# Weight tiles moved to 64 bytes beside the activation tiles, and the start of a hybrid decoder trunk put in another order

## The chip, the cores and the metric

The kernel runs on one core of one Trainium2 chip. The metric is device microseconds for one execution, from the launch on the device to its end. Lower is better.

## What is computed

Two layers of a decoder trunk over 256 positions of width 1024. Each layer makes a normed and conditioned h out of x, sends it through one large input projection, runs three branches (a gated linear recurrence, dilated window attention with rotary positions, gated linear attention), projects each back to the width, gates and adds them, and adds the product with `w_o` to x:

```python
mod = c_act @ ada_w + ada_b
shift, scale, gate = jnp.split(mod, 3, axis=-1)
h = rmsnorm(x, norm_g) * (1.0 + scale[:, None]) + shift[:, None]
z = h @ w_in
(a_x, a_g, b_q, b_k, b_v, b_g, c_q, c_k, c_v, c_g, m_g) = jnp.split(z, ...)
ya = rg_lru(causal_dwconv(a_x, conv_w, conv_b), lru_wa, lru_ba, lru_wx, lru_bx, lru_lambda)
ya = ya * jax.nn.silu(a_g)
q = rope(rmsnorm(b_q.reshape(shp), qn_g[:, None, :]), pos) * (HEAD_DIM ** -0.5)
k = rope(rmsnorm(b_k.reshape(shp), kn_g[:, None, :]), pos)
...
merged = mg[:, :, 0] * (ya @ proj_a) + mg[:, :, 1] * (yb @ proj_b) + mg[:, :, 2] * (yc @ proj_c)
return x + gate[:, None] * (merged @ w_o)
```

`rmsnorm` divides by the root of the mean square over the width; `rg_lru` uses softplus of a parameter; `rope` needs the cosine and sine of position times frequency. All weights are float32; with the conditioning weights `ada_w` they make up nearly all of the 168 MB that are read, each once.

## The kernel before

**Products.** To keep float32 accuracy, each factor is split into two parts in TensorE's rounded format: `whi` and `wlo` for weights, `hhi` and `hlo` for h, `yhi` and `ylo` for the branch results, `mhi` and `mlo` for the merged one. Every product is three matmuls into the same place (hi x hi, lo x hi, hi x lo). In the form of L797 to L799 (helper `mm_f`, 256 moving columns) the weights are loaded into the array and the activations stream; so also in L777 to L779 (gate of attention, `bg`). In the form of L789 to L791 (helper `mm_t`, 384, 400 or 512 moving columns) the activations are loaded and the weights stream; for q, k and v the loaded activations are every second column (`x[:, k, t::2]`).

**Units.** The weights come in units of up to 512 KB, 288 of them over two layers, in the order of a string: `a0 q1 k1 v1 k2 q2 v2 a1 q3 k3 v3 mA pA c0 c1 c2 c3 mC pC mB pB wo`, ahead of which q, k, v of pair 0 and bg run together. `advance` (from L206) keeps three units ahead: SP's queue loads `raw`, ACT makes `whi` (L223), DVE makes `wlo` (L224). Six `raw` buffers and four each of `whi` and `wlo` are in the pool `wts`. The rows of `ada_w` come between the units and are reduced on DVE (`ada_tile`, L325); at the start, sixteen of them come between the first units, since h needs them.

**Memory.** Tiles are laid out in SBUF pool after pool, in the order in which the pools are made: `one`, then `two`, then `wts`. By the addresses of the build, modulo 128 bytes: `whi` and `wlo` begin at 64; `hhi` and `hlo` (and `mhi` and `mlo`, under the same tags) at 32; `yhi` and `ylo` at 0.

**The start.** SP's queue issues the loads of `c_sb`, the identity, x in two halves, `vec_sb` (small vectors) and then the weights. ACT and DVE make `cact` (the SiLU of the conditioning), DVE `diag`, TensorE turns it into a row that stands on all partitions (L313), ACT copies it to `crow`, which `ada_tile` needs. `stats_start` squares x on ACT (four instructions, L372), adds on DVE (L375, L376) and sums over partitions with two matmuls of ones (L379). `rstd_full` makes the inverse root with a logarithm and an exponential on ACT and one Newton step on DVE (L341 to L348). `h_tile` makes h, eight tiles, each as soon as its two rows of `ada_w` are reduced (L357 `tmp`, L359 `hhi`, L360 `hlo`). The angles, sines and rotary tables of layer 0 (`angles`, `rope_tables`, L412 to L442) are asked for at unit 2 and wait for the last h tile written so far, `softplus` (L390 to L404) at unit 16; the loads that they need are issued on SP's queue behind unit loads. The order of instructions on each engine is that of a scheduler that models time, within these bounds.

Of the kernel before, what the change touches and what calls it, by code (L numbers as in the profile page):

```python
# [12 lines left out]
I32 = mybir.dt.int32  # L13
# [113 lines left out]
def hybrid_trunk(ctx: ExitStack, tc: tile.TileContext, ws, ada, vec, gates, a2, qkg, c_t, x_t, pos, inv, eye,  # L127
# [107 lines left out]
    pos_sb = one.tile([P, 2], I32, name="pos_sb")  # L235
# [21 lines left out]
    epsc = one.tile([P, 1], F32, name="epsc")  # L257
    V.memset(epsc, EPS)
    mhalf = one.tile([P, 16], F32, name="mhalf")
    V.memset(mhalf, -0.5)  # L260
    hpi = one.tile([P, 1], F32, name="hpi")
    V.memset(hpi, float(np.pi / 2))
    att_sb = one.tile([P, 3, P], F32, name="att_sb")
    G.memset(att_sb, 0.0)

# [33 lines left out]
    cact = one.tile([P, KT], F32, name="cact")  # L299
# [18 lines left out]
    mod = one.tile([P, L, 3, KT], F32, name="mod")  # L318
    acc = one.tile([P, L, 24], F32, name="acc")
# [31 lines left out]
    def h_alloc(l):  # L351
        return one.tile([P, KT, S], F32R, name="hhi", tag="hhi"), one.tile([P, KT, S], F32R, name="hlo", tag="hlo")
# [15 lines left out]
    def stats_start():  # L368
        sq = []
        for i, tag in enumerate(("cv", "csg", "co", "bv")):  # L370
# [12 lines left out]
    sp4 = one.tile([P, L, KT], F32, name="sp4")  # L383
    sp4n = one.tile([P, L, KT], F32, name="sp4n")
    hb = one.tile([P, L, 2 * KT], F32, name="hb")

    def softplus():
        lam = vec_sb[:, :, V_LAM:V_LAM + KT]
        e, s, s2, p = (one.tile([P, L, KT], F32, name=f"spl{i}") for i in range(4))
# [20 lines left out]
    def angles():  # L410
        pf, an, k = (one.tile([P, 2] if i == 0 else [P, 2, 32], F32, name=f"an{i}") for i in range(3))
# [128 lines left out]
    def evac_qk(l, nm, p, ps):  # L540
        i = 0 if nm == "q" else 1
        ro = two.tile([P, 2, 6, 64], F32, name="ro")
        ss = two.tile([P, 2, 6], F32, name="ss")
# [420 lines left out]
    def small():  # L964
        a, v = cur["h_last"]
        with tc.issue_after(a), tc.issue_after(v):
            softplus()
# [103 lines left out]
```

## Time and profile before

| | |
|---|---|
| three runs | 910.75, 912.31, 912.46 us; median 912.31 |
| the profiled execution | 912.47 us, of which span 910.7 us |
| granted TensorE clock, mean | 0.996 of full |
| TensorE (PE) busy | 872.9 us, 96% of the span, 6,340 matmuls |
| VectorE (DVE) busy | 673.0 us, 74% |
| ScalarE (ACT) busy | 532.0 us, 58% |
| GpSimd (POOL) busy | 175.1 us, 19% |
| read from HBM | 168.23 MB, 186 GB/s over the span |

The busy share says which engine has the least room. How long one matmul occupies the engine when others follow it is not its duration, since they are pipelined, but the distance from its start to the next start. The timeline (start, duration, engine, line, operation, tiles, and in brackets the idle time before it and what ended that) tells both. The view by windows gives busy time and counts of each engine in a stretch of the span.

### The profile page before, as it was taken

What the parts mean: (1) busy time and instruction counts of PE and PEld (TensorE: products, weight loads), DVE (VectorE), ACT (ScalarE), POOL (GpSimd) and SP (SyncE); (2) the same over time, 40 slices, a digit from 0 to 9 for tenths busy, and PEclk for the clock granted to TensorE, in tenths of its full rate; (3) what the DMA queues carried; (4) which work ended last, traced back from release to release, by engine and by line L of the source; (5) the groups of instructions that cost most, each with busy time, mean ns of one, the idle gap of its engine ahead of it and who ended that gap; (6) DMA issues with size and microseconds to landing.
All of it is one profiled execution on the core that took longest, in us unless ns stands there. A gap on an engine that the chain in (4) does not pass through costs nothing.

```text
span 910.7 us, 16407 instructions
## 1 busy us (share of the span) xinstructions
PE 872.9 (96%) x6340; PEld 825.3 (91%) x6340; DVE 673.0 (74%) x1115; ACT 532.0 (58%) x897; POOL 175.1 (19%) x160
## 2 busy tenths in 40 slices
PE   3989999999999999999999999989999999999998
PEld 3978999999988888999889999989999988899998
DVE  6998898669666667666775888986896666656674
ACT  4376976686644554634454689666874545554451
POOL 0026365124000110100030525551330001000000
PEclk9999999999999999999999999999999999999999
DMA  9884456446765666676655544563667565455651
GB/s 328 317 279 139 145 165 207 132 136 201 240 189 191 202 212 205 208 238 206 224 152 160 177 145 145 179 195 109 190 206 232 160 190 163 150 173 185 188 163 47
DMA packets 52111, 170.16 MB, mean 187 GB/s; under 512 B 6240, under 2 KB 8160, under 8 KB 52032
## 3 DMA queue, kind: packets, MB, share of 16 engines
q1 hardware_dynamic: 51216, 167.04, 57.7%
q10 hardware_dynamic: 672, 1.87, 0.7%
q8 instruction: 50, 0.82, 0.4%
q0 software_dynamic: 144, 0.20, 0.2%
q14 instruction: 29, 0.24, 0.1%
HBM read 168.23 MB, written 1.05 MB: 186 GB/s over the span
## 4 chain that ended last, share of the span: by engine, by line
PE 57%; DVE 18%; DMA 10%; issue 7%; ACT 5%; POOL 3%; SPq 0%; DVEq 0%; ACTq 0%
PE mm L797 10%; PE mm L799 10%; PE mm L798 10%; DMA raw<-in_ada_dram 8%; DVE wlo L224 7%; PE mm L791 6%; PE mm L790 6%; PE mm L789 6%; PE xps L172 1%; ACT whi L223 1%; POOL ss L560 1%; PE xps L168 1%; DVE raw L325 1%; DVE rb L554 1%; DVE ra L552 1%
## 5 line engine op out<-in xcount | busy, mean ns | idle before, releaser
L224 DVE TENSOR_TENSOR wlo<-raw,whi 128x1024 fp32r<-128x1024 f32 (+2 forms) x288 | 335.6, 1173 | 86.9 <-ACT whi L223 85.5
L223 ACT CAST whi<-raw 128x1024 fp32r<-128x1024 f32 (+2 forms) x288 | 280.2, 977 | 189.5 <-PE mm L798 123.6
L797 PE MATMUL mm<-hhi,whi 128*128 128x256 f32 x768 | 217.8, 284 | 3.3 <-DVE rb L554 3.2
L799 PE MATMUL mm<-hhi,wlo 128*128 128x256 f32 x768 | 216.6, 282 | 3.1 <-DVE wlo L224 3.1
L798 PE MATMUL mm<-hlo,whi 128*128 128x256 f32 x768 | 216.0, 281 | 0.0
L789 PE MATMUL mm<-whi,hhi 128*128 128x384 f32 (+2 forms) x480 | 170.9, 361 | 7.2 <-ACT hhi L359 6.5
L790 PE MATMUL mm<-wlo,hhi 128*128 128x384 f32 (+2 forms) x480 | 173.0, 362 | 1.4 <-DVE wlo L224 1.2
L791 PE MATMUL mm<-whi,hlo 128*128 128x384 f32 (+2 forms) x480 | 169.1, 358 | 0.5 <-DVE hlo L360 0.5
L797 PEld LDWEIGHTS mm<-hhi,whi 128*128 128x128 f32 x768 | 144.6, 188 | 5.3 <-ACT tmp L847 3.6
L799 PEld LDWEIGHTS mm<-hhi,wlo 128*128 128x128 f32 x768 | 144.5, 188 | 4.3 <-DVE wlo L224 3.7
L798 PEld LDWEIGHTS mm<-hlo,whi 128*128 128x128 f32 x768 | 144.8, 189 | 0.4
L789 PEld LDWEIGHTS mm<-whi,hhi 128*128 128x128 f32 x480 | 93.4, 195 | 15.3 <-ACT hhi L359 7.9
L790 PEld LDWEIGHTS mm<-wlo,hhi 128*128 128x128 f32 x480 | 93.9, 196 | 9.1 <-DVE wlo L224 2.8
L325 DVE CUSTOM_DVE_ANT_0 raw<-raw,crow,vec_sb 128x1024 f32<-128x1024 f32 x38 | 48.7, 1283 | 70.7 <-DMA raw<-in_ada_dram 70.7
L791 PEld LDWEIGHTS mm<-whi,hlo 128*128 128x128 f32 x480 | 92.7, 194 | 7.2 <-DVE hlo L360 0.8
L797 PE MATMUL mm<-yhi,whi 128*128 128x256 f32 x320 | 89.9, 281 | 2.1 <-DVE mg L939 2.1
L798 PE MATMUL mm<-ylo,whi 128*128 128x256 f32 x320 | 89.3, 279 | 0.0
L799 PE MATMUL mm<-yhi,wlo 128*128 128x256 f32 x320 | 89.2, 279 | 0.0
L797 PEld LDWEIGHTS mm<-yhi,whi 128*128 128x128 f32 x320 | 60.4, 189 | 3.1 <-DVE mg L939 2.3
L799 PEld LDWEIGHTS mm<-yhi,wlo 128*128 128x128 f32 x320 | 60.2, 188 | 0.8 <-DVE mrg L905 0.8
L798 PEld LDWEIGHTS mm<-ylo,whi 128*128 128x128 f32 x320 | 60.1, 188 | 0.0
L698 POOL TENSOR_TENSOR at_hl<-att_sb,at_hl 128x384 fp32r<-128x384 f32 x8 | 8.8, 1096 | 207.1 <-ACT at_hl L697 207.1
(236 smaller groups left out, 1408.0 us busy)
## 6 DMA issues: line engine op xcount, KB each, us to landing
raw<-in_ws_dram SPq DMA_DIRECT2D x192, 512.0 KB, 4.0
raw<-in_ws_dram SPq DMA_DIRECT2D x88, 384.0 KB, 3.2
raw<-in_ada_dram SPq DMA_DIRECT2D x38, 512.0 KB, 4.5
raw<-in_ws_dram SPq DMA_DIRECT2D x8, 400.0 KB, 5.4
g_raw<-in_gates_dram ACTq DMA_DIRECT2D x3, 512.0 KB, 4.9
x_sb<-in_x_t_dram SPq DMA_DIRECT2D x2, 512.0 KB, 6.7
ada_yhi<-in_ada_dram SPq DMA_DIRECT2D x2, 512.0 KB, 7.9
ada_ylo<-in_ada_dram SPq DMA_DIRECT2D x2, 512.0 KB, 9.1
```

The source lines that it names most:

```text
L168: seen[0] = T.matmul(*a, **k).ins
L172: seen[0] = T.transpose(*a, **k).ins
L223: A.copy(hi, r)
L224: V.tensor_tensor(lo, r, hi.bitcast(F32), ALU.subtract)
L325: V.tensor_tensor_reduce(w, w, crow2, 1.0, b, ALU.mult, ALU.add, a if i == 0 else m)
L552: V.tensor_tensor(ra.rearrange("p (g s) d -> p g s d", g=3), z4, ctab[l][:, i, t].unsqueeze(2).to_broadcast(bc), ALU.mult)
L789: T.matmul(o, ah, wh, start=(k == 0), stop=False)
L790: T.matmul(o, ah, wl, start=False, stop=False)
L791: T.matmul(o, al, wh, start=False, stop=(k == KT - 1))
L797: T.matmul(ps[:, 0:S], hi[:, a:b], xh[:, k], start=(k == 0), stop=False)
L798: T.matmul(ps[:, 0:S], hi[:, a:b], xl[:, k], start=False, stop=False)
L799: T.matmul(ps[:, 0:S], lo[:, a:b], xh[:, k], start=False, stop=(k == nk - 1))
```

## The change

It has two parts. The pools are made in another order, and some tiles move to other pools: `head` (small tiles), `wts`, `gap`, `mov` (`hhi`, `hlo`, `mhi`, `mlo`), `one`, `two`, `sml`. By the addresses of the build, modulo 128 bytes, `whi` and `wlo` still begin at 64, `hhi` and `hlo`, `mhi` and `mlo` now at 0, and `yhi` and `ylo` still at 0.

The second part is the start. The sum of squares is made by eight matmuls over the four squared tiles, without adds on DVE. The angles, the rotary tables of layer 0 and softplus stand in the code ahead of the sum of squares; their positions, frequencies and gains are loaded on ACT's queue at the start, into a tile of their own (`g0`, in the place of `pt1`). `vec_sb` is loaded ahead of x.

```diff
+    head = ctx.enter_context(tc.tile_pool(name="head", bufs=1))
+    wts = ctx.enter_context(tc.tile_pool(name="wts", bufs=LEAD + 1))
+    gap = ctx.enter_context(tc.tile_pool(name="gap", bufs=1))
+    mov = ctx.enter_context(tc.tile_pool(name="mov", bufs=1))
     one = ctx.enter_context(tc.tile_pool(name="one", bufs=1))
     two = ctx.enter_context(tc.tile_pool(name="two", bufs=2))
-    wts = ctx.enter_context(tc.tile_pool(name="wts", bufs=LEAD + 1))
+    sml = ctx.enter_context(tc.tile_pool(name="sml", bufs=1))
...
-    c_sb = one.tile([P, KT], F32, name="c_sb")
-    vec_sb = one.tile([P, L, V_N], F32, name="vec_sb")
+    vec_sb = head.tile([P, L, V_N], F32, name="vec_sb")
+    c_sb = head.tile([P, KT], F32, name="c_sb")
...
+    SY.dma_start(out=vec_sb, in_=vec)
     for i in range(2):
         SY.dma_start(out=x_sb[:, 4 * i:4 * i + 4], in_=x_t[:, 4 * i:4 * i + 4])
-    SY.dma_start(out=vec_sb, in_=vec)
...
+    g0 = one.tile([P, 2, 3, 64], F32, name="g0", tag="pt1")
+    for t, s in ((pos_sb, pos), (inv_sb, inv.partition_broadcast(P)), (g0, qkg[0].partition_broadcast(P))):
+        A.dma_start(out=t, in_=s)
...
-        return one.tile([P, KT, S], F32R, name="hhi", tag="hhi"), one.tile([P, KT, S], F32R, name="hlo", tag="hlo")
+        return mov.tile([P, KT, S], F32R, name="hhi", tag="hhi"), mov.tile([P, KT, S], F32R, name="hlo", tag="hlo")
...
-            if i % 2:
-                V.tensor_tensor(sq[i - 1], sq[i - 1], t, ALU.add)
-        V.tensor_tensor(sq[0], sq[0], sq[2], ALU.add)
         ps = xps()
-        for j in range(2):
-            T.matmul(ps[:, 0:S], ones, sq[0][:, j], start=(j == 0), stop=(j == 1))
+        for j in range(KT):
+            T.matmul(ps[:, 0:S], ones, sq[j // 2][:, j % 2], start=(j == 0), stop=(j == KT - 1))
...
-        gq = two.tile([P, 2, 3, 64], F32, name="gq", tag="pr", bufs=2)
-        load_after(None if l else ("sy", "a", 7), (gq, qkg[l].partition_broadcast(P)))
+        gq = g0
+        if l:
+            gq = two.tile([P, 2, 3, 64], F32, name="gq", tag="pr", bufs=2)
+            load_after(None, (gq, qkg[l].partition_broadcast(P)))
...
+    angles()
+    rope_tables(0)
+    softplus()
+    V.tensor_scalar(vec_sb[:, :, V_ON:V_ON + 2], vec_sb[:, :, V_ON:V_ON + 2], 0.5, None, ALU.mult)
     sts = stats_start()
...
-    sts = layer(0, h, {2: tables, 15: load_small, 16: small})
+    sts = layer(0, h, {15: load_small})
```

Left out of the diff: `mhi` and `mlo` move to `mov` like `hhi`; small tiles (`epsc`, `mod`, `acc`, `hb`, `cact`, the steps of softplus and some sums) move to `sml`; `sp4` and `sp4n` to `head` and `gap`; the closures `tables` and `small` go.

The scheduler's order at three places. First DVE at the very start, before the change: `cact`, `diag`, then the adds of the squares, then the first sums of `ada_w`.

```order
L303 TENSOR_SCALAR cact<-cact 128x8
L304 RECIPROCAL cact<-cact 128x8
L305 TENSOR_TENSOR cact<-cact,c_sb 128x8
L309 TENSOR_TENSOR diag<-eye_sb,cact 128x1024
L375 TENSOR_TENSOR sq<-sq 128x512
L307 TENSOR_SCALAR vec_sb<-vec_sb 128x2x8
L968 TENSOR_SCALAR vec_sb<-vec_sb 128x2x2
L375 TENSOR_TENSOR sq<-sq 128x512
L376 TENSOR_TENSOR sq<-sq 128x512
```

The same place on DVE after the change (`g_138` is the tile of the gains, `an` are the angles, `spl` the steps of softplus):

```order
L445 TENSOR_SCALAR g_138<-g_138 128x192
L428 SCALAR_TENSOR_TENSOR an_170<-an_171,an_170 128x64
L315 TENSOR_SCALAR cact<-cact 128x8
L399 TENSOR_SCALAR spl_197<-spl_196 128x16
L428 SCALAR_TENSOR_TENSOR an_170<-an_171,an_170 128x64
L316 RECIPROCAL cact<-cact 128x8
L400 RECIPROCAL spl_197<-spl_197 128x16
L430 TENSOR_SCALAR an_170<-an_170 128x64
L317 TENSOR_TENSOR cact<-cact,c_sb 128x8
L401 TENSOR_TENSOR spl_197<-spl_197,spl_196 128x16
L432 SCALAR_TENSOR_TENSOR an_171<-an_170 128x64
L321 TENSOR_TENSOR diag<-eye_sb,cact 128x1024
```

The adds are gone, and the gains, the angles and the first steps of softplus stand among and ahead of `cact` and `diag`.

Second, DVE around the first h tile, before the change:

```order
L347 TENSOR_TENSOR rs_q<-rs_q,rs_m 128x256
L348 SCALAR_TENSOR_TENSOR rs_y<-rs_q,rs_y 128x256
L224 TENSOR_TENSOR wlo<-raw,whi 128x800
L357 SCALAR_TENSOR_TENSOR tmp<-x_sb,mod,rs_y 128x256 x2
L224 TENSOR_TENSOR wlo<-raw,whi 128x768 x2
L360 SCALAR_TENSOR_TENSOR hlo<-tmp,mod,hhi 128x256 x2
```

and after it:

```order
L359 TENSOR_TENSOR rs_q<-rs_q,rs_m 128x256
L360 SCALAR_TENSOR_TENSOR rs_y<-rs_q,rs_y 128x256
L230 TENSOR_TENSOR wlo<-raw,whi 128x800
L230 TENSOR_TENSOR wlo<-raw,whi 128x768 x2
L369 SCALAR_TENSOR_TENSOR tmp<-x_sb,mod,rs_y 128x256 x2
```

Three subtractions of `wlo` stand between `rs_y` and the first `tmp`, where one stood.

Third, ACT from its first instruction to the first split weights, before the change:

```order
L301 ACT_TABLE_LOAD
L302 ACTIVATE cact<-c_sb 128x8
L372 ACTIVATE sq<-x_sb 128x512 x4
L314 COPY crow<-xps 128x512 x2
L341 ACTIVATE rs_y<-xps,epsc 128x256
L345 ACTIVATE rs_y<-rs_y 128x256
L223 CAST whi<-raw 128x800
```

and after it, from the load of the gains on:

```order
L276 DMA g_138<-in_qkg_dram 128x384
L313 ACT_TABLE_LOAD
L314 ACTIVATE cact<-c_sb 128x8
L398 ACTIVATE spl_196<-spl_196 128x16
L431 ACT_TABLE_LOAD
L431 ACTIVATE sn<-an_170 128x2x32
L433 ACTIVATE cs<-an_171,hpi 128x64
L384 ACTIVATE sq<-x_sb 128x512 x4
L326 COPY crow<-xps 128x512 x2
L353 ACT_TABLE_LOAD
L353 ACTIVATE rs_y<-xps,epsc 128x256
L357 ACT_TABLE_LOAD
```

Three table loads and the sines are new here; before the change two table loads stood further behind.

## Rows read from the trace of the kernel before

**Rows 1.** The page: busy time, share of the span, instructions of each engine.

```profile
PE 872.9 (96%) x6340; PEld 825.3 (91%) x6340; DVE 673.0 (74%) x1115; ACT 532.0 (58%) x897; POOL 175.1 (19%) x160
```

**Rows 2.** Timeline of PE, yhi in layer 1: start, us, engine, line, operation.

```profile
839.99 0.28 PE L797 MATMUL mm<-yhi,whi 128*128 128x256 f32 x1
...
842.71 0.28 PE L797 MATMUL mm<-yhi,whi 128*128 128x256 f32 x1
```

**Rows 3.** Timeline of PE, the same tiles in layer 0.

```profile
397.51 0.28 PE L797 MATMUL mm<-yhi,whi 128*128 128x256 f32 x1
...
400.34 0.28 PE L797 MATMUL mm<-yhi,whi 128*128 128x256 f32 x1
```

**Rows 4.** Timeline of PE, hhi in layer 1.

```profile
856.54 0.28 PE L797 MATMUL mm<-hhi,whi 128*128 128x256 f32 x1
...
857.01 0.28 PE L798 MATMUL mm<-hlo,whi 128*128 128x256 f32 x1
857.14 0.28 PE L799 MATMUL mm<-hhi,wlo 128*128 128x256 f32 x1
...
859.38 0.28 PE L797 MATMUL mm<-hhi,whi 128*128 128x256 f32 x1
```

**Rows 5.** Windows, L798: stretch, us, PE, PEld (count), PEclk, DMA, GB/s.

```profile
830.00:850.00 20.00, 16.22 (x60) 11.04 (x59) 1.00 0.63 194
387.00:407.00 20.00, 15.92 (x57) 10.62 (x57) 1.00 0.74 239
```

**Rows 6.** Timeline of PE, weights moving: 384 columns, layer 1, then 512.

```profile
601.37 0.34 PE L789 MATMUL mm<-whi,hhi 128*128 128x384 f32 x1
...
602.43 0.34 PE L789 MATMUL mm<-whi,hhi 128*128 128x384 f32 x1
...
730.06 0.39 PE L789 MATMUL mm<-whi,hhi 128*128 128x512 f32 x1
...
732.86 0.40 PE L789 MATMUL mm<-whi,hhi 128*128 128x512 f32 x1
```

**Rows 7.** Groups by line and form: count, busy, mean ns, idle before.

```profile
L797 PE MATMUL mm<-hhi,whi 128*128 128x256 f32 x768 | 217.8, 284 | 3.3 <-DVE rb L554 3.2
```

**Rows 8.** Windows, all engines: us, PE, PEld, DVE, ACT, POOL busy, PEclk, DMA, GB/s.

```profile
62.00:80.00 18.00, 13.32 (x105) 12.26 (x104) 18.00 (x37) 12.25 (x26) 13.21 (x13) 1.00 0.42 130
94.00:156.00 62.00, 61.18 (x364) 58.49 (x363) 56.41 (x86) 48.37 (x86) 31.58 (x28) 1.00 0.58 177
```

**Rows 9.** Timelines of DVE, PE and ACT at the start, put together here.

```profile
3.33 1.23 DVE L309 TENSOR_TENSOR diag<-eye_sb,cact 128x1024 f32<-128x1024 f32 x1
...
11.05 0.69 DVE L376 TENSOR_TENSOR sq<-sq 128x512 f32<-128x512 f32 x1
...
20.12 1.82 DVE L224 TENSOR_TENSOR wlo<-raw,whi 128x768 fp32r<-128x768 f32 x2
...
4.61 3.78 PE L313 MATMUL xps<-diag,ones 128*128 128x128 f32 x16 [4.61 <-DVE diag L309]
11.89 2.04 PE L379 MATMUL xps<-sq,ones 128*128 128x256 f32 x4 [3.50 <-DVE sq L376]
20.41 0.70 PE L789 MATMUL mm<-whi,hhi 128*128 128x400 f32 x1 [6.47 <-ACT hhi L359]
...
8.01 2.29 ACT L372 ACTIVATE sq<-x_sb 128x512 f32<-128x512 f32 x4 [5.36 <-DMA x_sb<-in_x_t_dram]
```

**Rows 10.** ACT's table load, DVE's first step of softplus, rotary products (min/median/max ns).

```profile
56.42 1.28 ACT L391 ACT_TABLE_LOAD   x1
...
59.54 0.16 DVE L390 SCALAR_TENSOR_TENSOR spl<-vec_sb 128x16 f32<-128x16 f32 x1
...
L440 DVE TENSOR_TENSOR ctab<-gq,cs x8: 350/352/354, 54.8 to 291.4; 128x192 f32<-128x192 f32 x8
```

**Rows 11.** Timeline of PE, its longest wait between 62 and 80 us.

```profile
69.66 0.36 PE L797 MATMUL mm<-hhi,whi 128*128 128x256 f32 x1 [2.61 <-DVE rb L554]
```

**Rows 12.** DMA issues: tile, queue, count, KB, us to landing.

```profile
gq<-in_qkg_dram ACTq DMA_DIRECT2D x1, 192.0 KB, 5.6
```

More of the change, by code (lines that the diff above doesn't have):

```diff
@@ L256, in hybrid_trunk @@
     V.memset(ones, 1.0)
-    epsc = one.tile([P, 1], F32, name="epsc")
+    epsc = sml.tile([P, 1], F32, name="epsc")
     V.memset(epsc, EPS)
-    mhalf = one.tile([P, 16], F32, name="mhalf")
+    mhalf = sml.tile([P, 16], F32, name="mhalf")
     V.memset(mhalf, -0.5)
-    hpi = one.tile([P, 1], F32, name="hpi")
+    hpi = sml.tile([P, 1], F32, name="hpi")
     V.memset(hpi, float(np.pi / 2))
@@ L296, in vcol @@
         return vec_sb[:, l, c:c + n]
-    cact = one.tile([P, KT], F32, name="cact")
+    cact = sml.tile([P, KT], F32, name="cact")
     crow = one.tile([P, KT, P], F32, name="crow")
@@ L315, in hybrid_trunk @@
     crow2 = crow.rearrange("p k n -> p (k n)")
-    mod = one.tile([P, L, 3, KT], F32, name="mod")
-    acc = one.tile([P, L, 24], F32, name="acc")
+    mod = sml.tile([P, L, 3, KT], F32, name="mod")
+    acc = sml.tile([P, L, 24], F32, name="acc")
     def ada_tile(l, c, w):
@@ L373, in stats_start @@
             sq.append(t)
[L374 to L376 removed]
         ps = xps()
[L378 to L385 removed]
+        for j in range(KT):
+            T.matmul(ps[:, 0:S], ones, sq[j // 2][:, j % 2], start=(j == 0), stop=(j == KT - 1))
+        return ps
+    hb = sml.tile([P, L, 2 * KT], F32, name="hb")
     def softplus():
         lam = vec_sb[:, :, V_LAM:V_LAM + KT]
[L389 removed]
+        e, s, s2, p = (sml.tile([P, L, KT], F32, name=f"spl{i}") for i in range(4))
         V.scalar_tensor_tensor(e, lam, -1.0, lam, ALU.mult, ALU.max)
@@ L410, in angles @@
     def angles():
-        pf, an, k = (one.tile([P, 2] if i == 0 else [P, 2, 32], F32, name=f"an{i}") for i in range(3))
+        pf, an, k = ((sml if i == 0 else one).tile([P, 2] if i == 0 else [P, 2, 32], F32, name=f"an{i}") for i in range(3))
         V.tensor_copy(pf, pos_sb)
@@ L542, in evac_qk @@
         ro = two.tile([P, 2, 6, 64], F32, name="ro")
-        ss = two.tile([P, 2, 6], F32, name="ss")
+        ss = sml.tile([P, 2, 6], F32, name="ss", bufs=2)
         for t in range(2):
@@ L586, in gen_att @@
             pss_t = [pss.tile([P, 512], F32, name="ps_s", tag="s") for _ in range(2)]
-            st = two.tile([P, 4], F32, name="st")
+            st = sml.tile([P, 4], F32, name="st", bufs=2)
             with order("B"):
@@ L704, in gen_co @@
         o = two.tile([P, 2, S], F32, name="co", bufs=1)
-        ms = two.tile([P, 2], F32, name="cms")
+        ms = sml.tile([P, 2], F32, name="cms", bufs=2)
         ps = xps()
@@ L933, in layer @@
                 if p == 0:
-                    mhl = (one.tile([P, KT, S], F32R, name="mhi", tag="hhi"), one.tile([P, KT, S], F32R, name="mlo", tag="hlo"))
+                    mhl = (mov.tile([P, KT, S], F32R, name="mhi", tag="hhi"), mov.tile([P, KT, S], F32R, name="mlo", tag="hlo"))
                 for e in range(2):
@@ L955, in hybrid_trunk @@
     cur["rstd"], cur["h"] = rstd, h
-    def tables():
-        a, v = cur["h_last"]
-        with tc.issue_after(a), tc.issue_after(v):
-            load_after(("sy", "a", 3), (pos_sb, pos), (inv_sb, inv.partition_broadcast(P)))
-            angles()
-            rope_tables(0)
[L964 to L967, printed above, removed]
-        V.tensor_scalar(vec_sb[:, :, V_ON:V_ON + 2], vec_sb[:, :, V_ON:V_ON + 2], 0.5, None, ALU.mult)
-    sts = layer(0, h, {2: tables, 15: load_small, 16: small})
+    sts = layer(0, h, {15: load_small})
     rstd = rstd_full(sts, 4)
```

4 lines of the change are left out of this document (3 added, 1 removed).

## Prediction

> **What bounds the kernel now.** I read the page's busy line first: PE is busy for 96% of the span, DVE for 74%, ACT for 58% [rows 1]. So the time is TensorE's time except where something makes it wait, and the next question is how fast the matmuls follow one another. A matmul's own duration (0.28 us) does not tell this, since matmuls are pipelined; the distance between two starts does. I took it from the timeline of PE, over 24 matmuls of 256 columns in a row, and it is not the same everywhere. With the activations yhi and ylo, in layer 1: 839.99 to 842.71, that is 2.72 / 24 = 113.3 ns [rows 2]. With the same tiles and the same code in layer 0: 2.83 / 24 = 117.9 ns [rows 3]. With hhi and hlo: 2.84 / 24 = 118.3 ns, and there the single steps wander, one of them from 857.01 to 857.14 [rows 4]. Over 20 us around the two stretches with yhi one matmul line starts 60 and 57 times, and the granted clock is 1.00 in both [rows 5], so it is not the clock. Over all stretches with yhi I read about three fifths at the fast step and two fifths at the slow one, and use that as an estimate. Those with hhi never settle at the fast one.
>
> By the addresses of the two builds, whi and wlo begin 64 bytes past a multiple of 128 before the change, yhi and ylo at a multiple of 128, hhi and hlo (and mhi and mlo, in the same place) 32 past one. So the pairs that are 64 apart are the only ones that show the fast step, and the pairs that are 32 apart do not. After the change whi and wlo still begin 64 past, and hhi, hlo, mhi and mlo, like yhi and ylo, at a multiple: every large product gets the distance that so far only the y products have.
>
> The second stretch is the start. DVE does everything there: from 62 to 80 us it is busy for 18.00 of 18.00 us, PE for 13.32 [rows 8]; PE waits 2.61 us at 69.66 for DVE [rows 11].
>
> **Part 1, the addresses.** The matmuls concerned with 256 moving columns of activations: 3 x 768 with hhi and hlo [rows 7], 3 x 128 with mhi and mlo and 192 in bg, from the code; 2,880. If they go as the y products do, three fifths at 113.3 and two fifths at 117.9, the mean is 115.1, so 3.2 ns each [rows 2 to 4]: 9.2 us. The bounds are 0.4 ns (all at the slow step) and 5.0 ns (all at the fast one). For 512 columns (384 matmuls, from the code) the step is 2.80 / 12 = 233.3 ns [rows 6]; twice 113.3 would be 226.7, so 6.7 at most, and three fifths of that is 4.0: 1.5 us. For q, k and v the activations are the stationary operand and read with a stride of two, the weights stream; 1.06 / 6 = 176.7 ns [rows 6], one and a half times 113.3 would be 170.0. [...] With 960 of them and 192 more of 384 or 400 columns in the units of the first pair, from the code: 1,152 x 1.5 = 1.7 us. Together 12.4 us.
>
> Not all of that arrives. From 94 to 156 us DVE is busy for 56.41 of 62 us beside a full PE [rows 8]: the weights are split by ACT and DVE just ahead of their use there, and a PE that is 2 to 3% faster meets unsplit weights. I take 2 us off for those stretches. Elsewhere the split weights lie ready several us before PE needs them, and DVE at 74% and ACT at 58% hide the rest [rows 1]. Part 1 is worth 10.4 us.
>
> A rule speaks against this part. The Trainium skill, in "TensorE: Matmul & The Clock Gate", section "Step-by-step: what each phase is for", says that PE has two independent SBUF read ports and that loading the next weights takes no bandwidth from the running matmul. By it the addresses should not matter, and the sum would be part 2 alone. The trace does not agree in one respect: the same form of matmul runs at 113.3 and at 118.3 ns at a full clock [rows 2, 4]; but no row shows that the addresses are the reason, and so what the rule says is rival D below.
>
> **Part 2, the start.** *Losses.* The sum of squares goes from 2 to 8 matmuls. The trace shows 4 passes for 2 of them, 2.04 us, begun at 11.89 behind the last add [rows 9], so 16 passes now, at 0.51 each 8.2 us. They need not wait for the adds; the squares come one by one from 8.01 on, 2.29 us for four [rows 9]; begun at about 8.6 the passes end at about 16.8 instead of 13.93, and at about 15 if later passes take half as long: +1 to +2.9. Behind it the logarithm and the exponential now each load a table on ACT because Sin came between; such a load is 1.28 us [rows 10]. The first is hidden under the wait for PE, the second is on the way to rs_y: +1.3. On DVE two more subtractions of wlo, 1.82 us [rows 9], now stand ahead of the first tmp, behind which hhi and the first matmul wait. Against this, they no longer stand between the first tmp and the first hlo. The three DMAs of positions, frequencies and gains are issued on ACT's queue at once instead of behind the unit loads on SP; the gains' like took 5.6 us to land [rows 12], and since DVE works in order, the scaling of the gains ahead of cact holds back cact, diag and the crow that all ada sums need: diag, now at 3.33 [rows 9], begins 2 to 4 us later, and PE's first 3.78 us with it; part of that comes before the squares are there and costs nothing. The vector load ahead of x on SP costs some tenths. Together, the first main matmul, now at 20.41 [rows 9], moves to about 22.5 to 26.5.
>
> *Gains.* The three adds of 0.69 us [rows 9] go: 2.07 us of DVE, most of it on the way. More important, 39 operations leave DVE between 34 and 80 us: eight products for the rotary tables at 352 ns [rows 10], 2.8 us, and 31 small ones (11 for the angles, 1 scaling, 19 for softplus) at some 0.14, as the first of softplus with 0.16 [rows 10], 4.3 us; about 7 us. Two table loads of 1.28 leave ACT there as well. PE's waits in that stretch, the one of 2.61 us [rows 11] the largest of some, are what DVE's lateness turns into, and as DVE is full, 7 us less of work in front of it can bring nearly 7 us of earlier ends. What comes late next is the ada stream, which DVE has to reduce and which loads beside the weights; DVE stays full there either way.
>
> The start thus loses 2 to 6 and wins 2 (if only the waits of PE go) to 8. Bounds: 6 won, 4 lost; I take 2 won, since DVE's work really leaves a full stretch while much of the later start falls where PE had waited for DVE anyway.
>
> **Sum.** The profiled run took 912.47 us, 910.7 of them span; the median of the three is 912.31, so the profile may stand for it. 912.47 - 10.4 - 2 = 900.1; I say 900.
>
> **Rivals.** (B) The new layout holds the fast step everywhere, in all three forms: 2,880 x 5.0 + 384 x 6.7 + 1,152 x 6.7 = 24.7 us, less 2 for DVE, and 2 from the start: 888. For it: 24 steps in a row without one slip [rows 2]. Against: layer 0 with the same addresses [rows 3]. (C) The products settle at the slow step: 2,880 x 0.4 = 1.2, and 2 from the start: 909. For it: rows 3, and that layer 0's DMA load, 0.74 against 0.63, lies beside it [rows 5]. (D) The distance does nothing, and h differs from y for another reason: only the start is left, 910.5. It is what the rule of the Trainium skill's "TensorE: Matmul & The Clock Gate" would give. (F) The addresses pay as forecast, but the start is 4 us worse: 906. (E) Slower: the new distance makes PE settle at a bad step instead of wandering. The longest single steps with hhi are near 0.123 us, one of 0.13 by the rounded starts [rows 4]; if that became the lasting step, 4.7 ns x 2,880 = 13.5 us lost, 2 won at the start: 924. It decides as soon as the mean step is above 119.0 ns (118.3 plus 2 us / 2,880). Against it: no stretch with y shows it.
>
> **How the numbers follow.** A, the forecast (893 to 906): 0.50. B: 0.14. C: 0.14. D: 0.10. F: 0.05. E: 0.07. The range runs from B's middle to D's edge, 886 to 910, and leaves out E and most of D. About 0.2% is what a measurement here can tell from no change, 910.5 to 914.1. Below: A, B, F, nearly all of C and a little of D, 0.83; within: the rest, 0.10; above: 0.07.
>
> **What would show it.** The timeline of PE with hhi in layer 1: 24 steps in 2.72 us for A or B where they are settled, 2.84 for D, 2.95 for E; the count of one matmul line in 20 us goes from 57 to 60. With whi against hhi of 384 columns: 6 steps in 1.06 if this form gains nothing, 1.02 if all. At the start: the first main matmul after 22.5, DVE with idle time between 62 and 80 us and no wait for rb near 70. Part 2 is wrong if the first main matmul is later than 26.5 or DVE is as full from 34 to 80 as before. The forecast is wrong if the mean step with hhi is above 117 or below 114.

## The result, and the profile after

The changed kernel takes 918.7 us, the kernel before 911.54 us (medians of 15 runs each); the ratio is 1.0074, interval 1.006 to 1.0087. Two of the 15 runs of the changed kernel, 954 and 1,422 us at granted clocks of 0.85 and 0.56, do not count in the ratio. The forecast was 900 us, with a chance of 0.07 for slower. The profiled execution of the changed kernel took 914.62 us (span 912.8) and lies at the low end of its runs, so its trace shows some 2 us of the 7; the rest is known from timed comparisons only.

The page's busy line, to be held against [rows 1], shows no difference that would explain anything: PE is as busy as before.

```profile
PE 871.6 (95%) x6352; PEld 825.8 (90%) x6352; DVE 671.0 (74%) x1112; ACT 533.3 (58%) x898; POOL 178.1 (20%) x160
```

**The start.** The timelines of PE, DVE and ACT from 8 to 27 us, each engine in its own fence, answer to [rows 9].

```profile
11.46 3.78 PE L325 MATMUL xps<-diag,ones 128*128 128x128 f32 x16 [11.46 <-DVE diag L321]
15.03 3.74 PE L388 MATMUL xps<-sq,ones 128*128 128x256 f32 x16
26.25 0.70 PE L798 MATMUL mm<-whi,hhi 128*128 128x400 f32 x1 [7.47 <-ACT hhi L371]
```

```profile
8.23 0.18 DVE L319 TENSOR_SCALAR vec_sb<-vec_sb 128x16 f32<-128x16 f32 x1 [3.35 <-DMA vec_sb<-in_vec_dram]
...
10.18 1.22 DVE L321 TENSOR_TENSOR diag<-eye_sb,cact 128x1024 f32<-128x1024 f32 x1
...
15.90 1.28 DVE L337 CUSTOM_DVE_ANT_0 ada_yhi<-ada_yhi,crow,vec_sb 128x1024 f32<-128x1024 f32 x1 [0.24 <-ACT crow L326]
...
22.19 0.42 DVE L360 SCALAR_TENSOR_TENSOR rs_y<-rs_q,rs_y 128x256 f32<-128x256 f32 x1
22.53 2.72 DVE L230 TENSOR_TENSOR wlo<-raw,whi 128x800 fp32r<-128x800 f32 x3
25.17 0.88 DVE L369 SCALAR_TENSOR_TENSOR tmp<-x_sb,mod,rs_y 128x256 f32<-128x256 f32 x2
```

```profile
18.81 0.48 ACT L353 ACTIVATE rs_y<-xps,epsc 128x256 f32<-128x256 f32 x1 [1.65 <-PE xps L388]
19.30 1.28 ACT L357 ACT_TABLE_LOAD   x1
20.60 0.42 ACT L357 ACTIVATE rs_y<-rs_y 128x256 f32<-128x256 f32 x1
```

DVE waits 3.35 us for the small vectors, and `cact` and `diag` stand behind that wait in its order; diag comes at 10.18 instead of 3.33, and the first sum of `ada_w` (L337) at 15.90. The sum of squares follows on PE behind diag and ends at 18.77 instead of 13.93; the exponential's table load of 1.28 us and the three `wlo` come between it and the first `tmp`; the first main matmul begins at 26.25 instead of 20.41. In the window from 22.2 to 32.2 us the granted clock is 0.50 (1.2 GHz, the lower of its two levels), PE having had nothing from 18.77 to 26.25 (columns as in [rows 8]):

```profile
22.20:32.20 10.00, 5.95 (x19) 5.92 (x20) 10.00 (x16) 2.88 (x5) 0.00 (x0) 0.50 1.03 418
62.00:80.00 18.00, 14.08 (x107) 13.25 (x105) 15.98 (x23) 12.42 (x26) 9.83 (x9) 1.00 0.55 182
94.00:156.00 62.00, 60.12 (x370) 57.78 (x369) 53.54 (x79) 49.74 (x85) 32.02 (x24) 1.00 0.55 162
```

From 62 to 80 us DVE has room now, 15.98 of 18 us, but PE still waits there, 0.89 us at 70.67 and 1.71 at 75.45 for `rb` and 1.57 at 80.31 for ACT: 4.17 us together, where the kernel before had three waits of 4.58 us together, the 2.61 us of [rows 11] the longest.

**The steps.** The timeline of PE, matmuls of one line 24 steps apart: first h in layer 1 where it is fast, then h where it is slow, then y, then six steps of 384 columns.

```profile
613.10 0.28 PE L806 MATMUL mm<-hhi,whi 128*128 128x256 f32 x1
...
615.82 0.28 PE L806 MATMUL mm<-hhi,whi 128*128 128x256 f32 x1
...
858.47 0.28 PE L806 MATMUL mm<-hhi,whi 128*128 128x256 f32 x1
...
861.30 0.28 PE L806 MATMUL mm<-hhi,whi 128*128 128x256 f32 x1
...
841.51 0.28 PE L806 MATMUL mm<-yhi,whi 128*128 128x256 f32 x1
...
844.33 0.28 PE L806 MATMUL mm<-yhi,whi 128*128 128x256 f32 x1
...
602.61 0.34 PE L798 MATMUL mm<-whi,hhi 128*128 128x384 f32 x1
...
603.67 0.34 PE L798 MATMUL mm<-whi,hhi 128*128 128x384 f32 x1
```

h does reach 2.72 / 24 = 113.3 ns, in places, which it never did before; but in most places it settles at 2.83 / 24 = 117.9. And y in layer 1, fast before [rows 2], is slow now (2.82 / 24 = 117.5), at the same distance from its weights modulo 128. 384 columns stand at 1.06 / 6 = 176.7, as before [rows 6]. I took all steps between two neighbouring starts of these products out of both traces (those below 127 ns) and counted which are 114 ns or shorter:

| | h, mean step | h, share fast | m, mean | m, share | y, mean | y, share | 384 columns | 512 columns |
|---|---|---|---|---|---|---|---|---|
| before | 118.29 | 0.00 | 118.30 | 0.00 | 115.12 | 0.61 | 176.4 | 233.2 |
| after | 116.74 | 0.24 | 117.78 | 0.00 | 116.95 | 0.19 | 177.0 | 233.4 |

h gains 1.55 ns on each of 2,304 matmuls, 3.6 us; m and bg 0.3; y gives back 1.83 ns x 960 = 1.8 us; 384 columns another 0.6. About 1.5 us are left, where 12.4 were forecast.

### The profile page after: what moved, and what is told of

Same layout as the page of the kernel before. It is cut to its first block, busy times and chain, and to the rows that moved or that the text cites. A ratio compares the mean times of both kernels' runs of the same rounds, so it can differ in the third digit from the quotient of the medians.

```text
span 912.8 us, 16433 instructions
## 1 busy us (share of the span) xinstructions
PE 871.6 (95%) x6352; PEld 825.8 (90%) x6352; DVE 671.0 (74%) x1112; ACT 533.3 (58%) x898; POOL 178.1 (20%) x160
## 4 chain that ended last, share of the span: by engine, by line
PE 55%; DVE 16%; DMA 13%; issue 7%; ACT 5%; POOL 3%; DVEq 0%; SPq 0%; ACTq 0%
DMA raw<-in_ada_dram 11%; PE mm L806 10%; PE mm L808 10%; PE mm L807 10%; DVE wlo L230 8%; PE mm L798 5%; PE mm L799 5%; PE mm L800 5%; POOL ss L569 2%; ACT whi L229 2%; PE xps L178 1%; PE xps L174 1%; DVE rb L563 1%; DVE ra L561 1%; DVE raw L337 1%
## 5 line engine op out<-in xcount | busy, mean ns | idle before, releaser
L798 PE MATMUL mm<-whi,hhi 128*128 128x384 f32 (+2 forms) x480 | 171.4, 361 | 7.5 <-ACT hhi L371 7.5
L798 PEld LDWEIGHTS mm<-whi,hhi 128*128 128x128 f32 x480 | 93.6, 196 | 14.2 <-ACT hhi L371 7.9
L337 DVE CUSTOM_DVE_ANT_0 raw<-raw,crow,vec_sb 128x1024 f32<-128x1024 f32 x38 | 48.7, 1283 | 68.1 <-DMA raw<-in_ada_dram 68.1
```

Of the source, the lines that this page charges most:

```text
L337: V.tensor_tensor_reduce(w, w, crow2, 1.0, b, ALU.mult, ALU.add, a if i == 0 else m)
L798: T.matmul(o, ah, wh, start=(k == 0), stop=False)
```

## The experiments

Two questions: which part of the change costs the 7 us, and why the addresses gave so little.

**Which part: the layout alone, and the start alone.** `e1_pools` is the changed kernel with the start put back; `e2_start` the kernel before with the new start, `h` kept at 32 past a multiple of 128. `e3_squares` is `e1_pools` with the sum of squares on TensorE and the vectors loaded ahead of x. The edit of `e1_pools` against the full change, shortened, with comments added:

```diff
-    SY.dma_start(out=vec_sb, in_=vec)          # ahead of x
+    SY.dma_start(out=vec_sb, in_=vec)          # behind x
-    g0 = one.tile([P, 2, 3, 64], F32, name="g0", tag="pt1")
...
+                V.tensor_tensor(sq[i - 1], sq[i - 1], t, ALU.add)
...
-    angles()
-    rope_tables(0)
-    softplus()
+    sts = layer(0, h, {2: tables, 15: load_small, 16: small})
```

> The changed layout of tiles (weights 64 bytes beside h, modulo 128) with the start as it was before the change. Theory S (the start is the loss: DVE waits in order for the small vectors ahead of cact, so the first main matmul moved from 20.41 to 26.25 us): this kernel has its first main matmul at about 20.4 and is 1 to 4 us faster than before the change, some 908 to 911 us. Theory A (the layout is the loss): it is slower than before the change by 5 us or more, like the full change. In the trace, both see 24 matmuls with hhi either in about 2.72 or in about 2.83 us.

> The changed start alone; weights and h stay 32 bytes apart modulo 128, as before the change. Theory S: first main matmul at about 26.2 us, 5 to 9 us slower than before the change, some 917 to 921 us. Theory A: within 2 us of before the change, since the late start is made good later. In the trace, 24 matmuls with hhi take 2.84 us everywhere.

> The changed layout, the sum of squares on TensorE without the adds and the small vectors loaded ahead of x, but angles, tables and softplus where they were before the change. Theory S: cact and diag are early again, the first main matmul comes between 20 and 22 us, and the time is within 2 us of e1_pools. If the eight matmuls themselves were the delay, the first main matmul would come at about 23 or later and the time lie nearer to the full change.

Measured: `e1_pools` 911.95 us against 912.3, ratio 1.0004 (0.9987 to 1.0021). `e2_start` 916.64, ratio 1.0057 (1.0034 to 1.008). `e3_squares` 909.44, ratio 0.998 (0.9961 to 1.000). The first main matmul of `e1_pools` begins at 20.24, as before the change. So the start costs some 5 us and the layout neither costs nor gains anything that can be measured; together they give the full change within the intervals (1.0004 x 1.0057 = 1.0061 against 1.0074). Theory A is out, and so is the idea that the eight matmuls delay the start. Of theory S the size for the layout (1 to 4 us gained) was at most its lower end. The first main matmuls, from the timeline of PE in `e2_start`, then that of PE and three lines of DVE's in `e3_squares`:

```profile
26.92 0.70 PE L792 MATMUL mm<-whi,hhi 128*128 128x400 f32 x1 [7.25 <-ACT hhi L363]
```

```profile
4.57 3.78 PE L321 MATMUL xps<-diag,ones 128*128 128x128 f32 x16 [4.57 <-DVE diag L317]
9.13 3.72 PE L384 MATMUL xps<-sq,ones 128*128 128x256 f32 x16 [0.78 <-ACT crow L322]
19.09 0.70 PE L792 MATMUL mm<-whi,hhi 128*128 128x400 f32 x1 [6.24 <-ACT hhi L367]
```

```profile
3.29 1.22 DVE L317 TENSOR_TENSOR diag<-eye_sb,cact 128x1024 f32<-128x1024 f32 x1
5.53 0.18 DVE L315 TENSOR_SCALAR vec_sb<-vec_sb 128x16 f32<-128x16 f32 x1 [1.01 <-DMA vec_sb<-in_vec_dram]
...
10.63 1.29 DVE L333 CUSTOM_DVE_ANT_0 ada_yhi<-ada_yhi,crow,vec_sb 128x1024 f32<-128x1024 f32 x1 [4.86 <-ACT crow L322]
```

The sixteen passes run from 9.13 here, beside the squares, and the first main matmul comes 1.3 us earlier than before. In `e2_start` h stays at a mean step of 118.28 with none fast, and y at 0.62 fast, as in the kernel before: the start does not touch the steps. The small vectors are loaded ahead of x in `e3_squares` too, but they are there at 5.5 us, 3.9 us after their issue, and in the full change at 8.2, 6.6 us after it. Beside them only the three loads on ACT's queue (positions, frequencies, gains) are new in the full change, so these make DVE's wait longer: the four kernels that have them (the full change, `e2_start`, `e4_behind_diag`, `e7_tables`) have the vectors at 7.8 to 8.2 us, `e3_squares`, `e5_softplus` and `e6_squares_old` without them at 5.5.

**Which piece of the start.** `e4_behind_diag` keeps the full change but issues everything that was moved behind `diag`; `e6_squares_old` is the squares and the vector load alone in the old layout; `e5_softplus` is `e3_squares` with softplus early too; `e7_tables` is the full change with softplus put back late.

```diff
+    with tc.issue_after(cur["diag"]):          # e4_behind_diag, against the full change, shortened
+        angles()
+        V.tensor_scalar(b1, b1, 1.0, None, ALU.add)
+        rope_tables(0)
+        softplus()
```

```diff
-    sts = layer(0, h, {2: tables, 15: load_small, 16: small})
+    softplus()                                 # e5_softplus, against e3_squares: ahead of stats_start
+    sts = layer(0, h, {2: tables, 15: load_small})
```

> The full change, with the angles, tables and softplus issued behind diag on their engines, so that cact and diag no longer stand behind the operations that wait for the small vectors. Theory S (this wait is what made the start late): diag begins near 3.4 us again, the first main matmul at 21 to 24 us, and the time is 4 to 8 us below the full change, 910 to 915 us. If the order on DVE is not the cause (the eight matmuls or the table loads are): first main matmul after 25 us and a time within 2 us of the full change's 918.7.

> The kernel before with the sum of squares on TensorE and the small vectors loaded ahead of x, and the old layout. If e3_squares gained by its start (its first main matmul came at 19.09 us against 20.41): 909 to 911 us, the same gain of about 2 us. If it gained by the layout: no difference from before the change.

> e3_squares with softplus too made at the start (behind diag on DVE, no further table on ACT), the angles and rotary tables still later. If the moved work of DVE is what delays the start: first main matmul later than 21 us and slower than e3_squares by 2 us or more. If it is the angles and tables with their loads and ACT's Sin: first main matmul at 19 to 20 us, and the time within 2 us of e3_squares, 908 to 911 us; one table load and 19 operations then leave the stretch from 54 to 62 us.

> The full change with softplus back where it was; angles and rotary tables still at the start. If the angles and tables are what delays the start: first main matmul at 25 us or later, and 915 to 920 us, like the full change. If softplus is: 909 to 912 us.

| | time | ratio to before | first main matmul |
|---|---|---|---|
| e4_behind_diag | 915.79 us | 1.0043 (1.0028 to 1.0058) | 26.47 us |
| e6_squares_old | 911.82 us | 0.9991 (0.9975 to 1.0007) | 20.32 us |
| e5_softplus | 910.9 us | 0.9982 (0.9963 to 1.0002) | 19.33 us |
| e7_tables | 918.13 us | 1.0076 (1.0056 to 1.0096) | 25.86 us |

`e7_tables` against `e5_softplus` settles it: the angles and rotary tables, with their three loads, are the whole loss, softplus costs nothing measurable early. `e4_behind_diag` was to show that DVE's wait for the vectors is the mechanism, and missed: diag comes at 4.40 us there and the first main matmul still at 26.47. The timelines of ACT and DVE say why:

```profile
10.39 1.15 ACT L383 ACTIVATE sq<-x_sb 128x512 f32<-128x512 f32 x2
11.45 0.57 ACT L325 COPY crow<-xps 128x512 f32<-128x512 f32 x1
12.03 1.28 ACT L430 ACT_TABLE_LOAD   x1
13.32 0.26 ACT L430 ACTIVATE sn<-an 128x64 f32<-128x64 f32 x1
13.48 0.33 ACT L432 ACTIVATE cs<-an,hpi 128x64 f32<-128x64 f32 x1
13.72 0.56 ACT L325 COPY crow<-xps 128x512 f32<-128x512 f32 x1
```

```profile
13.84 0.63 DVE L450 TENSOR_TENSOR stab<-g,sn 128x192 f32<-128x192 f32 x2
...
16.08 1.27 DVE L336 CUSTOM_DVE_ANT_0 ada_yhi<-ada_yhi,crow,vec_sb 128x1024 f32<-128x1024 f32 x1
```

The second `crow` copy, for which all sums of `ada_w` wait, now stands behind the sine's table load, and the squares begin at 9.15 instead of 8.01 because x lands later. On DVE the eight products of the rotary tables run from 13.84 to 16.08, ahead of the first sum of `ada_w`. That sum begins at 16.08 here, at 15.90 in the full change and at 10.63 in `e3_squares`. Put ahead of `diag` the tables hold up DVE, put behind it they hold up ACT and then DVE; either way the rows of h are late. The time lies some 3 us below the full change all the same (ratios 1.0043 and 1.0074, intervals apart); what gained them is not shown. Nor do these runs separate what the loads cost from what the operations cost. `e6_squares_old` had its first main matmul at 20.32, not near 19, and its interval spans no change and the 2 us that were expected; with `e3_squares` it leaves open whether the squares alone gain anything.

**Why the addresses gave little.** The first two probes run products on TensorE alone, at the four distances; `p1_distance` enters each group behind a pause, `p2_entry` behind transposes.

The loop of both, shortened:

```python
for k in range(8):       # groups of 24; d is 0, 32, 64 or 96 bytes
    T.matmul(ps[:, 0:256], wh[k], xh[k] + d, ...)
    T.matmul(ps[:, 0:256], wh[k], xl[k] + d, ...)
    T.matmul(ps[:, 0:256], wl[k], xh[k] + d, ...)
```

> TensorE alone, a probe that leaves out the whole computation but some products: groups of 72 matmuls in the kernel's form (weights loaded, 256 columns of activations moving) with the activations 0, 32, 64 and 96 bytes past the weights modulo 128, six entries each, then 384 columns with a strided stationary operand, then 512. If the distance alone sets the step: 113.3 ns at 64, about 118 at 0, 32 and 96, in every entry. If the entry decides: at 64 some entries at 113.3 and some at 117.9. If neither matters without other engines at work: one step at all four distances.

> TensorE alone again (a probe, only some products are computed): groups of 72 matmuls, weights loaded and 256 columns of activations moving, at 0, 32, 64 and 96 bytes modulo 128, but now each group is entered without a pause from one to eight transposes, as the kernel enters many of its products. Theory L (at 64 apart two steps are stable and the entry decides): at 64 some groups run at about 113.3 ns from start to end and the others at about 117.8; at 96, the distance that h had before the change, all wander around 118.4. Rival theory N (other engines and transfers make the difference): all groups at 64 at about 117.8, as in p1_distance.

At 96, where h lay before (activations minus weights is -32), all groups wander around 118.3 to 118.9 ns, single steps from 113 to 125, like the kernel's. At 64 they settle at 117.8, slow, whatever the entry (two of the eight in `p2_entry` end mixed, at 117.1); none settled at 113.3. So the distance alone is not the condition, and the probe seemed to speak for other engines. But its tiles did not lie as the kernel's do in all respects, which the next two probes put right: `p3_addresses` uses the kernel's places modulo 128 and the kernel's spacing of hi and lo parts, `p4_spacing` varies the spacing.

> TensorE alone (a probe, only some products are computed), with weights and activations at the addresses of the kernel modulo 128, as pairs weights/activations: 64/0 (all products after the change), 64/32 (h before it), 0/64, 0/0, 64/64, 0/32, 32/0, 96/0; hi and lo parts as far apart as in the kernel; each pair entered in six ways (a pause, one, two and four transposes, three products of 64 rows, three of 384 columns), 48 matmuls each. Theory L (the entry decides between two lasting steps): at 64/0 some of the six groups lie at 113.3 to 114 ns and the others near 117.8; at 64/32 none does. Theory N (something outside TensorE decides): at 64/0 all near 117.8.

> TensorE alone, as p3_addresses, only pairs 64/0 and 0/64, with the lo part of the weights 16384 or 4096 bytes behind the hi part and the lo part of the activations 8192 or 8320 bytes behind, six entries each. In p1_distance and p2_entry (4096 and 8320, pair 0/64) no group settled at 113.3 ns, in p3_addresses (16384 and 8192) five of six did. If the spacing is the reason: fast groups at 16384 and 8192 only, few or none at 4096 and 8320. If it is chance of the entry: fast groups in all four.

In `p3_addresses`, of six groups at 64/0 one lies at 113.3 ns and five at 117.8; at 0/64, the same distance with the sides exchanged, five at 113.3 and one at 117.8; at the six other pairs no group settles at 113.3 (means 116.7 to 120.0; 120.0 for h's old pair 64/32). So the fast step needs no other engine, and theory N falls. `p4_spacing` repeats it: of twelve groups at 0/64 nine are fast when the lo part of the activations lies 8192 bytes behind the hi part, none of twelve at 8320; the spacing of the weights makes no difference (four of six and five of six). The first two probes had 8320. But 8320 is 8192 + 128: by the addresses of the build it also moves the lo part from 64 to 192 modulo 256, beside weights at 128. So this may be the place modulo 256 that is found below, and not the spacing; no run separates the two.

**The sides exchanged in the kernel.** `e8_swapped` is `e5_softplus` with the tiles 64 bytes on (shown is what the edit adds to `e5_softplus`):

```diff
+    mhalf = head.tile([P, 16], F32, name="mhalf")
-    mhalf = sml.tile([P, 16], F32, name="mhalf")
```

> e5_softplus with every tile 64 bytes further on: weights at a multiple of 128, all activations 64 past one, so the same distance with the sides exchanged; no instruction moves. Theory L (the entry decides, and with the pair 0/64 most entries end at the fast step, as five of six groups in p3_addresses against one of six at 64/0): well over half of the units of 24 matmuls take 2.72 us instead of 2.83, and the time falls by 4 to 9 us, to 902 to 907 us. If only the distance counts: the same as e5_softplus within 1.5 us, 909 to 912 us, with one unit in five or fewer at 2.72.

Measured 907.24 us, ratio 0.9959 (0.994 to 0.9979). The time lies just above the range expected, but the reason given for it does not hold: the share of fast steps is 0.21 with h and 0.30 with y, about as in `e5_softplus` (0.21 and 0.25), not over a half. Its interval and that of `e5_softplus` overlap, so what it gains over that is not told apart from nothing. The expectation rested on five of six groups on TensorE alone; the kernel does not follow them.

**What sets the share.** Two ideas were left: that y takes its step over from the products ahead, or that more of the address than modulo 128 counts. `p5_before` puts h, 32 or 0 past a multiple, right ahead of y. Its y tile lay at 128 modulo 256, with weights at 192; its h tile at 0 modulo 256.

> TensorE alone, hi and lo spaced as in the kernel. First part, ten times each: one to three groups of 24 matmuls with h 32 past a multiple of 128 (as before the change) or 0 past one (as after it), weights 64 past, and right behind them, without a pause, 48 matmuls with y at a multiple of 128. Before the change three fifths of y's steps were fast, after it one fifth, though y and the weights kept their distance. Theory L (y takes its step over from the entry): behind h at 0, y keeps h's lasting step from the first matmul on, slow behind slow; behind h at 32, which has no lasting step, y ends at the fast step in some of the ten and at the slow one in others. If something else than the products ahead decides: the same share in both. Second part: groups at 64/0 and 0/64 broken by four transposes ahead of the first, second or third matmul of a triple; if the place in the triple decides, the fast step follows one of the three places in all four entries.

The timeline of PE has each group of 48 as one row: X is h, Y is y. A group of 48 takes 5.62 us from first start to last end when fast, 5.82 to 5.90 when slow, 5.99 when it wanders.

```profile
107.69 5.90 PE L183 MATMUL mm<-X,W 128*128 128x256 f32 x48
113.43 5.62 PE L183 MATMUL mm<-Y,W 128*128 128x256 f32 x48
118.91 5.99 PE L183 MATMUL mm<-X,W 128*128 128x256 f32 x48
124.74 5.82 PE L183 MATMUL mm<-Y,W 128*128 128x256 f32 x48
130.53 6.00 PE L183 MATMUL mm<-X,W 128*128 128x256 f32 x48
136.37 5.62 PE L183 MATMUL mm<-Y,W 128*128 128x256 f32 x48
```

Behind slow h, y is fast in ten of ten (113.43 is one); behind wandering h in seven of ten. So at this place y does not take over the step of the products ahead, and the theory that this sets y's share is out here; y's place after the change, 64/0, was not tried in it. X and Y both lie 64 from the weights modulo 128; they differ modulo 256: weights at 192 with activations at 128 settle fast, 17 of 20; weights at 192 with activations at 0 settle slow, 33 of 34 in this run. The place in the triple at which a group is broken shows no effect: at weights 128 and activations 64, 21 of 24 entries are fast, and of the broken ones 4, 3 and 4 of 4 by place.

**That place in the kernel.** Modulo 256, the kernel before had the y products at 192 (weights) and 128, its fast ones. The change left the distance and moved them to 64 and 0; h went to 64 and 128. So modulo 128 only h and m moved, the weights and y not; modulo 256 all did. `e9_mod256` is `e5_softplus` with all large products at 192 and 128, by moving small tiles between pools (the edit against `e5_softplus`, shortened, with comments added):

```diff
+    mhalf = head.tile([P, 16], F32, name="mhalf")
-    inv_sb = one.tile([P, 32], F32, name="inv_sb")      # from where it stood
+    inv_sb = one.tile([P, 32], F32, name="inv_sb")      # to 11 lines further down
-        e, s, s2, p = (sml.tile([P, L, KT], F32, name=f"spl{i}") for i in range(4))
+        e, s, s2, p = ((head, gap, gap, sml)[i].tile([P, L, KT], F32, name=f"spl{i}") for i in range(4))
```

> e5_softplus with tiles shifted so that all large products lie as y and its weights lay before the change modulo 256 too: weights at 192, all activations at 128 (so activations minus weights is 192 modulo 256; in the full change h lies at plus 64 and y at minus 64, weights at 64). No instruction of TensorE moves. On TensorE alone the pair at 192/128 took the fast step behind 17 of 20 groups, at 192/0 hardly ever. Theory M (the place modulo 256 sets how often the fast step is reached): three fifths or more of the steps with h, m and y at 114 ns or less, means at or below 115.1, and a time 5 to 12 us below e5_softplus, 899 to 905 us: the gain that the prediction had put on the change. Rival: only the distance modulo 128 and chance count: a quarter fast as in e5_softplus, 909 to 912 us.

Measured 903.26 us against 911.99, ratio 0.991 (0.9891 to 0.9929): faster than both kernels. The mean steps and shares, counted as above: h 114.93 ns, 0.64 fast; m 113.34, 1.00; y 113.60, 0.95; 384 columns 174.0 and 512 columns 230.4. Compared with `e5_softplus` (h 116.85 and 0.21; m 117.79 and 0.00; y 116.69 and 0.25; 176.9; 233.4) only addresses differ. For y not even the distance differs: by the addresses of the builds it begins 58,048 bytes behind the first `whi` in `e5_softplus`, `e8_swapped` and `e9_mod256` alike, and its share is 0.25, 0.30 and 0.95. So for y it is the place that counts, not the distance.

One trace's share is partly chance. In the six traces with the addresses of the full change h has 0.14 to 0.24, y 0.19 to 0.28, m 0.00 five times and 0.45 once (`e1_pools`); at the old addresses y has 0.61, 0.62 and 0.77 (`e6_squares_old`). The shares of `e9_mod256` lie above all of these. But h stays at 0.64 at the place where m has 1.00, so the place is not all; what else counts for h is not shown.

The windows of one matmul line (columns as in [rows 5]) and the timeline of PE with y, 24 steps apart:

```profile
830.00:850.00 20.00, 16.28 (x59) 11.02 (x60) 1.00 0.63 196
850.00:870.00 20.00, 16.22 (x60) 11.03 (x59) 1.00 0.64 195
387.00:407.00 20.00, 16.22 (x60) 11.06 (x59) 1.00 0.70 226
```

```profile
833.98 0.28 PE L800 MATMUL mm<-yhi,whi 128*128 128x256 f32 x1
...
836.70 0.28 PE L800 MATMUL mm<-yhi,whi 128*128 128x256 f32 x1
```

60 starts in 20 us from 387 to 407 us, where the kernel before had 57 [rows 5], beside nearly as much DMA traffic (226 GB/s against 239).

## Why the prediction was wrong

**What bounds the kernel** was read rightly: PE's steps set the time, and a step that is a few ns shorter is worth microseconds. `e9_mod256` shows the price. Against the kernel before, its steps save 3.36 ns x 2,304 with h, 4.96 x 384 with m, 1.52 x 960 with y, 2.4 x 1,056 and 2.8 x 384 with 384 and 512 columns: 14.7 us, of which 8.7 arrive between the medians (with the squares and softplus early, which gained nothing measurable by themselves).

**Part 1 failed at one step**: "the pairs that are 64 apart are the only ones that show the fast step", and from there "every large product gets the distance that so far only the y products have". The first half is true of the trace; the second took the distance modulo 128 for the whole condition. With the distance given, h came to a share of 0.24 instead of 0.61, and y, whose distance had not changed, fell from 0.61 to 0.19. Nothing in the trace of before could have told that 128 is the modulus, since it holds one fast pair and one wandering pair, and these differ modulo 256 as well (192/128 and 192/160); but the addresses of the builds would have shown that y's own place moves from 192/128 to 64/0. The term of 9.2 us measured 3.9 (3.6 for h, 0.3 for m and bg); y, which was put at nothing, measured -1.8; the 1.5 and 1.7 us for 512 and 384 columns measured -0.1 and -0.6. No run shows the 1.5 ns that the sum takes for 384 columns: measured were 0.6 ns lost in the change and 2.4 won in `e9_mod256`. The rule of the Trainium skill that was weighed there ("TensorE: Matmul & The Clock Gate", "Step-by-step: what each phase is for": loading weights takes nothing from the running matmul) gave the better number for part 1 here. But what the prediction drew from it, that addresses should not matter, is not what the runs show: in `p5_before`, on TensorE alone, ten of ten groups settle at 117.8 ns with X at 0 and 17 of 20 at 113.3 with Y, and `e9_mod256` differs from `e5_softplus` in addresses only. By which way the addresses act no run shows.

**Part 2 was nearly right in its losses and wrong in its gains.** Its failed step is "7 us less of work in front of it can bring nearly 7 us of earlier ends": 2 us won net were forecast, and `e2_start` lost some 5. The losses were put at 2 to 6 us with a first main matmul at 22.5 to 26.5; it came at 26.25, near the late end. The mis-sized term is diag, 2 to 4 us later as forecast, 6.85 measured. The mechanism, DVE waiting in order for a load, was right, but the load that ended the wait was that of the small vectors, at 8.23, while the gains, there at about 8.3 (6.7 us from their issue at 1.64), were used at 9.02 without a wait. The page of before lists the vectors at 6.8 us to landing, and the prediction had put their move ahead of x at some tenths. Another 1.95 us went to the operations of angles, gains, softplus and `cact` between that wait and diag, most of which had no price. The price of the table load (+1.3) and of the two `wlo` (+1.8) stand in the timeline as forecast. That the late end of the range nearly held is partly luck, since two of its terms were off in opposite ways: the squares' passes, put at +1 to +2.9 us by themselves, were not the delay (in `e3_squares` they end at 12.85, before the 13.93 of the kernel before). The gains failed: DVE did get free, 15.98 us busy in 18 where it had been full, but this gave back 1.7 us by the first unit of the ax and ag products (5.84 late at the first main matmul, 4.1 at 66.5 us) and 3.1 by 94 us, and most was lost again by 156 us, where PE has two new waits for `wlo`:

```profile
136.74 0.45 PE L799 MATMUL mm<-wlo,hhi 128*128 128x384 f32 x1 [0.61 <-DVE wlo L230]
...
150.54 0.46 PE L799 MATMUL mm<-wlo,hhi 128*128 128x384 f32 x1 [1.04 <-DVE wlo L230]
```

At the next stage, at 160 us, it is 4.8 us late once more. `e2_start`, which has no gain by addresses, is 5.2 us late there and still 4.2 at 804 us. The failed step took a full engine for the cause of all lateness there; `e3_squares` leaves the tables and softplus late and loses nothing, and `e5_softplus`, which takes softplus off that stretch, gains nothing over it.

**The rivals.** C (the slow step, 909) was nearest for part 1, but no case had C together with a late start; F's late start (4 us worse) was joined to a full gain. The two were priced apart and never added: 912.47 - 1.2 + 4 = 915, near the profiled 914.62 and still 3 to 4 us below the median. E, the only slower case, named a mechanism that nothing shows.

**What stays open.** Why the timed runs of the full change lie 4 us above its profiled one: the trace of one execution does not say; the profiles of `e2_start` and `e7_tables`, with the same start, lie at their medians or 1 us above (916.67 and 919.24). And why 192/128 settles fast in the kernel and 128/64 (0.30 with y in `e8_swapped`) mostly not, although on TensorE alone both do: other pairs modulo 256 were not tried in the kernel.

## What to carry to other kernels

Where matmuls with fresh weights follow one another at full clock, take the step between starts from the timeline for each pair of operands and set it beside their addresses; if it differs for the same form, the layout is worth percents, and the place that runs fast has to be copied whole (here modulo 256), not only the distance. Work moved into a start to relieve a later stage must be followed along each engine's order, ACT's tables included: here the same operations, with their loads, cost nothing in one place and 5 us in the other. An early load also delays those that are under way beside it, here by 2.7 us. And when two parts of a change are uncertain in opposite ways, price their bad ends together.

## What was not expected of the hardware

- The same matmul with its weight load has two lasting steps on TensorE alone, 113.3 and 117.8 ns at 256 columns, and which one lasts depends on where both operands lie, on more than the address modulo 128, and on where the alternating lo part lies (8192 bytes behind the hi part: nine of twelve groups fast; 8320, so at another place modulo 256: none). At the six other pairs of `p3_addresses` the groups lie at 116.7 to 120.0 ns.
- A step, once reached, can last as long as the row of products is not broken: in the changed kernel's trace the slow step holds from an entry at 819 us to the end of the products at 909, some 770 matmuls with h, y and m, which cost 3.5 us. It need not: in `p5_before` the step changes from 117.8 to 113.3 without a break where Y follows X.
- A table load on ACT cost 1.30 us from its start to the start of the next instruction (19.30 to 20.60), nothing more.
- Three loads of together about 0.2 MB on another queue moved the landing of the small vectors from 3.9 to 6.6 us after their issue.
